# One decoder layer on one core: the input projection issued in a written order, slot by slot, on all five queues

## The chip, the core and the metric

The kernel runs on one core of a Trainium2 chip. A core has a matrix engine (PE, with a weight load that overlaps it, PEld), a vector engine (DVE), a scalar engine (ACT), GpSimd (POOL) and SyncE (SP); SP and POOL issue most of the DMAs. Each engine takes its own instructions strictly in order and waits on semaphores for the others. The metric is the device time of one execution in microseconds, as the median of several runs; lower is better.

## The reference, cut to what matters

One layer: a normalised input `h` is projected to 7168 columns, which feed a convolution branch and a recurrence branch; both are gated, merged, projected and added to the input; a squared-ReLU MLP and a last normalisation follow. Sequence 1024, model width 1024, float32.

```python
z = jnp.einsum("bsd,de->bse", rms_norm(x, g_mix), w_in) + b_in
va, ga, xb, gb, sa, sb = jnp.split(z, cuts, axis=-1)   # 1024,1024,1536,1536,1024,1024
u = causal_depthwise_conv(va * jax.nn.sigmoid(ga), conv_a_w, conv_a_b)   # width 31
y_a = silu(layer_norm(u, ln_g, ln_b)) @ w_a_out
v = causal_depthwise_conv(xb, conv_b_w, conv_b_b)                        # width 4
v = rg_lru(v, ...)       # two block-diagonal gates of 16 heads of 96, then a scan in position
y_b = (v * gelu(gb)) @ w_b_out
m = sigmoid(sa) * y_a + sigmoid(sb) * y_b
x = x + m @ w_o
x = x + square(relu(rms_norm(x, g_mlp) @ w_1)) @ w_2
return rms_norm(x, g_final)
```

## The kernel before, in words

**Numbers.** Every matrix product is made of three passes in a reduced float format: each operand is split into a high and a low part, and high*high, high*low and low*high are accumulated. A low part is made in one of two ways: `split` (L54) copies on ACT and subtracts on DVE; `split_dma` (L67) writes minus the source on ACT (L69), adds the source by an accumulating POOL DMA (L70), and copies the high part on ACT (L71).

**Stages, in order of time.** (1) The opening normalises `x` and computes the first three column chunks (of 128 columns) of the projection (L305 to L372, an order written by hand). (2) The rest of the first 28 chunks: 12 of `xb`, 8 pairs `va`/`ga`; this is `zchunk` (L384), 48 matmuls of 128x128 by 128x512 for each of 25 chunks, called from the loop L597. Beside it run the recurrence: width-4 convolution (`xb_chunk`, L399), split (`rnn_load`, L423), 16 heads with 12 matmuls each (`rnn_gates`, L443), exponentials, tanh, roots and the scan (`rnn_scan`, L464); and the width-31 convolution `conv` (L522), some 48 DVE instructions for each of eight tiles. (3) The other 28 chunks, `gb`, `sa`, `sb`, in 14 pairs; each pair is a 2x2 block product with seven block products instead of eight (L637 to L743): `z_load` brings two raw tiles, `z_lhs` forms the sums on DVE and splits them, `z_mm` does 12 matmuls, `z_out` applies gelu or sigmoid. That is 98 steps, in the order `zseq` (L727). The right-hand sums (`x_sums`, `x_parts`) are prepared at the end of stage 2. (4) `yb` (L816), the layer normalisation (L780), `ya` (L830), the output projection, the MLP up (L1103, L1239) and down (L1310) stages and the last rows.

**What sets the order.** Where the code stands in `manual_schedule` (the opening, the start of the up stage, the down stage) PE, ACT and DVE issue in the order of the program text. Everywhere else, stages 2 and 3 among them, the library's scheduler orders each queue: it simulates the program with its timeline model (`schedule_with_timeline_sim=True`, L1486) and issues by priority what is ready in that model; `high_priority` (L402, L455, L508, L705) and `high_priority(-LOWP)` (L541) move the priorities.

**Memory.** Activations take 35 tiles of 4 KB a partition (`acts`, L36). Stage 2 has pools for weights (L42), heads (L126) and head weights (L127), in this order of addresses; stage 3 opens its pools (L621 to L625) over the same addresses: eight tiles of 4 KB for raw and split weights, then sums, then evacuated blocks. In PSUM stage 2 has three tiles of two banks for chunks and two of one bank for the heads.

Of the kernel before, what the change touches and what calls it, by code (L numbers as in the profile page):

```python
# [9 lines left out]
F32 = mybir.dt.float32  # L10
# [5 lines left out]
P = 128  # L16
# [14 lines left out]
def trunk_kernel(ctx: ExitStack, tc: tile.TileContext, x, xt_in, vecs, w_in, w_a_out, w_b_out,  # L31
# [4 lines left out]
    tp = ctx.enter_context(tc.tile_pool(name="acts", bufs=35))  # L36
# [5 lines left out]
    wp = stage.enter_context(tc.tile_pool(name="weights", bufs=2))  # L42
# [7 lines left out]

    def PS2(name):
        return pp.tile([P, HS], F32, tag="half", name=name, bufs=2)
# [73 lines left out]
    qp = stage.enter_context(tc.tile_pool(name="heads", bufs=6))  # L126
    rp = stage.enter_context(tc.tile_pool(name="head_w", bufs=2))  # L127

# [3 lines left out]
    def H(name, dt=F32):  # L132
        return qp.tile([HD, S], dt, tag="h", name=name)
# [29 lines left out]
    def load_w0(i):  # L163
        if i < 2:
            raw0.append(load_w(w_in[16 + i], f"w{i}"))
        else:
            raw0.append(T(f"w{i}_raw").rearrange("p (k c) -> p k c", c=P))
            nc.sync.dma_start(raw0[i], w_in[16 + i])
# [52 lines left out]
    def x_spread(hf):  # L221

        rb[hf] = PS2(f"rb{hf}")
# [81 lines left out]
    with tc.manual_schedule(engines={mybir.EngineType.Activation, mybir.EngineType.DVE,  # L305
# [15 lines left out]
        x_root(0, lambda: first_w(0, "h"))  # L321
        x_spread(0)
# [59 lines left out]
    zc = [0]  # L382

    def zchunk(ci):  # L384
        zc[0] += 1
        if zc[0] <= N0:
            return z0[zc[0] - 1]
        ws = get_w(w_in[ci], f"win{ci}", 100 if zc[0] < 5 else None)
        ps = PS(f"z{ci}")
        mm3(ps, [w + xw[k] for k, w in enumerate(ws)])  # L390
        return ps
# [7 lines left out]
    def xb_chunk(t):  # L399
        ps = zchunk(XB + t)  # L400
        a = T(f"xb{t}")
        with tc.high_priority():  # L402
            nc.scalar.activation(a, ps, AF.Identity, bias=bin_c[:, XB + t:XB + t + 1])  # L403
# [4 lines left out]
        for d in range(1, WB):  # L408

            w = WB - 1 - d  # L410
            nc.vector.scalar_tensor_tensor(v[:, d:S], a[:, 0:S - d],  # L411
                                           cbw_c[:, w * 12 + t:w * 12 + t + 1], v[:, d:S],
                                           ALU.mult, ALU.add)
        vt[t] = v
# [8 lines left out]
    def rnn_load(n):  # L423

        g, hh = divmod(n, 4)
        parts[n] = H(f"vh{n}", F32R), H(f"vl{n}", F32R)
        for (ti, p0, p1, d0) in PIECES[hh]:
            t = 3 * g + ti
            if t not in vp_:
                vp_[t] = T(f"vth{t}", F32R), T(f"vtl{t}", F32R)  # L430
                split(vt[t], *vp_[t])
# [54 lines left out]
    def rnn_steps():  # L486
        for n in range(-2, NH):
            if n >= 0:
                rnn_gates(n)
# [1001 lines left out]
```

## Time and profile before

| | |
|---|---|
| median of 3 runs | 1679.08 us (1678.63 to 1680.56) |
| the profiled execution | 1677.35 us |
| its span, first to last instruction | 1675.6 us |
| PE busy in it | 1588.4 us, 6910 matmuls |
| DVE, ACT, POOL busy | 1114.5, 886.3, 205.9 us |
| mean granted PE clock | 0.98 |

A matmul overlaps the next one, so a busy PE is not yet a PE at its pace: what counts is how long a stretch takes against its number of matmuls. "Idle before" is the time in which an engine stood still ahead of an instruction, with what ended it. Times in the views count from the start of the span.

### The profile page before, as it was taken

To read this page: it belongs to the slowest core of one execution; us is meant where nothing else is said; L and a number is where in the kernel's file an instruction comes from. 1 tells how busy PE (TensorE), PEld (TensorE's weight loads), DVE (VectorE), ACT (ScalarE), POOL (GpSimd) and SP (SyncE) were. 2 spreads that over 40 slices of the span, in tenths; PEclk is the share of its full clock that TensorE was granted. 3 is DMA by queue.
4 is the path that set the end of the run, shared out by engine and by line. 5 is a ranking of instruction groups with operands and counts; after the bars stand their busy time and mean duration, and the time that the engine had idled before them with its cause. 6 is when DMAs were issued, how large, how long until landed. Compare 5 with 4: busy or idle time off the path is not lost.

```text
span 1675.6 us, 18924 instructions
## 1 busy us (share of the span) xinstructions
PE 1588.4 (95%) x6910; PEld 1291.3 (77%) x6910; DVE 1114.5 (67%) x1488; ACT 886.3 (53%) x1184; POOL 205.9 (12%) x276
## 2 busy tenths in 40 slices
PE   8997989996899999999999999999999999999997
PEld 6875767774677777878788888788888888888875
DVE  6785988686998983324633224875555467888896
ACT  5548776583555656633553315654444466555542
POOL 0000000001222333311111100000000001111110
PEclk9998999998899999999999999999999999999999
DMA  9657776858578778857577542532333569888852
GB/s 368 159 138 205 185 189 174 219 146 244 124 185 230 199 197 227 213 175 219 133 207 176 150 157 89 158 126 102 125 113 114 161 232 235 214 222 209 209 113 101
DMA packets 97710, 299.15 MB, mean 179 GB/s; under 512 B 11424, under 2 KB 12960, under 8 KB 97616
## 3 DMA queue, kind: packets, MB, share of 16 engines
q1 hardware_dynamic: 62832, 193.36, 34.7%
q0 software_dynamic: 34640, 104.32, 28.8%
q8 instruction: 54, 0.88, 0.2%
q14 instruction: 40, 0.33, 0.1%
q10 hardware_dynamic: 144, 0.26, 0.0%
HBM read 146.11 MB, written 54.53 MB: 120 GB/s over the span
## 4 chain that ended last, share of the span: by engine, by line
PE 62%; issue 11%; DMA 8%; ACT 4%; DVE 3%; POOL 1%; SPq 0%; POOLq 0%; ACTq 0%; DVEq 0%
PE d L1275 13%; PE ya L95 5%; PE yb L95 4%; PE o L874 3%; PE e L1390 3%; PE z L95 3%; PE keep L1275 2%; PE o L95 2%; DMA zo<-zs 2%; DMA zo<-zw 1%; DMA g<-g 1%; PE o L898 1%; DMA yn<-yd 1%; DMA win_l<-win_raw 1%; DMA wb2a_raw<-in_w_b_out_dram 1%
## 5 line engine op out<-in xcount | busy, mean ns | idle before, releaser
L95 PE MATMUL z<-xh,win_h 128*128 128x512 f32 x400 | 125.1, 391 | 3.0 <-ACT xb L403 2.1
L95 PE MATMUL z<-xl,win_h 128*128 128x512 f32 x400 | 124.3, 391 | 0.0
L1287 DVE TENSOR_TENSOR acc<-acc,d 128x1024 f32<-128x1024 f32 x72 | 87.7, 1220 | 33.4 <-PE d L1275 32.8
L95 PE MATMUL z<-xh,win_l 128*128 128x512 f32 x400 | 99.2, 401 | 4.0 <-DMA win_l<-win_raw 4.0
L95 PEld LDWEIGHTS z<-xh,win_l 128*128 128x128 f32 x400 | 77.8, 195 | 21.3 <-DMA win_l<-win_raw 4.4
L95 PEld LDWEIGHTS z<-xh,win_h 128*128 128x128 f32 x400 | 74.8, 188 | 21.1 <-ACT xb L403 2.6
L95 PEld LDWEIGHTS z<-xl,win_h 128*128 128x128 f32 x400 | 75.4, 189 | 16.4
L548 DVE SCALAR_TENSOR_TENSOR y<-u,vec,y 128x498 f32<-128x498 f32 (+14 forms) x120 | 86.5, 740 | 0.3 <-ACT y L539 0.3
L548 DVE SCALAR_TENSOR_TENSOR yt<-u,vec,yt 128x499 f32<-128x499 f32 (+13 forms) x112 | 83.0, 741 | 0.0
L548 DVE SCALAR_TENSOR_TENSOR y<-yt,csum,y 128x499 f32<-128x499 f32 (+13 forms) x112 | 82.9, 740 | 0.0
L456 ACT ACTIVATE g<-rg,vec 96x512 f32<-96x512 f32 x64 | 41.3, 678 | 42.2 <-PE rg L454 17.3
L70 POOL DMA_DIRECT2D win_l<-win_raw x25 | 21.5, 859 | 333.2 <-ACT win_l L69 273.6
L1008 ACT ACTIVATE o<-s 128x512 fp32r<-128x512 f32 x64 | 38.1, 621 | 32.5 <-DVE s L1000 27.8
L1008 ACT ACTIVATE o<-w_raw 128x512 fp32r<-128x512 f32 x40 | 24.9, 624 | 51.2 <-DVE o L922 51.2
L411 DVE SCALAR_TENSOR_TENSOR v<-xb,vec,v 128x1023 f32<-128x1023 f32 (+2 forms) x36 | 45.7, 1279 | 5.0 <-ACT v L406 4.7
L823 DVE TENSOR_TENSOR m<-yb,sb 128x1024 f32<-128x1024 f32 x8 | 9.8, 1223 | 55.9 <-PE yb L95 55.9
L70 POOL DMA_DIRECT2D db_1l<-wr x7 | 6.0, 859 | 330.4 <-ACT db_1l L69 269.6
L452 PE MATMUL rg<-vh,rgh 96*96 96x512 f32 x64 | 27.9, 435 | 18.7 <-ACT g L456 18.6
L922 DVE TENSOR_TENSOR o<-s,o 128x512 fp32r<-128x512 f32 x64 | 42.4, 684 | 3.8 <-ACT o L1008 3.8
L906 DVE TENSOR_TENSOR x<-xr,o 128x1024 f32<-128x1024 f32 x8 | 9.7, 1219 | 51.9 <-PE o L874 37.7
L70 POOL DMA_DIRECT2D zo<-zw x42 | 36.4, 866 | 37.0 <-ACT zo L69 34.0
L121 ACT ACTIVATE xn<-x 128x1024 f32<-128x1024 f32 x8 | 8.5, 1057 | 58.8 <-DVE x L906 58.8
(1586 smaller groups left out, 4694.2 us busy)
## 6 DMA issues: line engine op xcount, KB each, us to landing
fr<-fd SPq DMA_DIRECT2D x32, 512.0 KB, 5.4
wr<-in_w_dram SPq DMA_DIRECT2D x32, 512.0 KB, 5.3
w_raw<-in_w_dram SPq DMA_DIRECT2D x31, 512.0 KB, 3.7
zw<-in_w_in_dram SPq DMA_DIRECT2D x28, 512.0 KB, 5.7
win_raw<-in_w_in_dram SPq DMA_DIRECT2D x25, 512.0 KB, 4.5
win_l<-win_raw POOLq DMA_DIRECT2D x25, 512.0 KB, 4.9
zo<-zw POOLq DMA_DIRECT2D x42, 256.0 KB, 4.1
fd<-fa SPq DMA_DIRECT2D x16, 512.0 KB, 3.3
```

Of the source, the lines that this page charges most:

```text
L70: nc.gpsimd.dma_start(l, src, accum_op=ALU.add)
L95: nc.tensor.matmul(ps[:, HALVES[hf]], a, b[hf], start=i == 0, stop=i == len(todo) - 1)
L411: nc.vector.scalar_tensor_tensor(v[:, d:S], a[:, 0:S - d], cbw_c[:, w * 12 + t:w * 12 + t + 1], v[:, d:S], ALU.mult, ALU.add)
L452: nc.tensor.matmul(o, gh[:, gi, :], vh[:, hs], start=True, stop=False)
L456: nc.scalar.activation(a[:, hs], o, AF.Sigmoid, bias=(ba_c, bx_c)[gi][:, n:n + 1])
L548: nc.vector.scalar_tensor_tensor(o[:, k:], a[:, 0:HS - k], c, o[:, k:], ALU.mult, add)
L874: nc.tensor.matmul(ps[:, HALVES[hf]], tok(a, k, t), wo[k][b][:, HALVES[hf]], start=k == 0 and b == 0 and n == 0, stop=k == 7 and b == 1)
L922: tt(l, src, h.bitcast(F32), ALU.subtract)
L1008: nc.scalar.activation(o[:, 0], src, AF.Copy)
L1275: nc.tensor.matmul(o, a, b, start=n == 0 and (p != 1 or g == 0), stop=n == len(todo) - 1, skip_group_check=p == 1 and g > 0)
L1287: tt(acc[p, q2], acc[p, q2], ps, ALU.add)
L1390: nc.tensor.matmul(o, a, b, start=n == 0, stop=n == len(todo) - 1)
```

## The change

Stages 2 and 3 are written as two loops inside `manual_schedule` for all five engines. Stage 2 is a loop over 25 slots, one chunk each. A slot issues: the load of the chunk after next; 36 of the 48 matmuls; the first gate of the previous head and the matmuls of its second gate; the other 12 matmuls; the first-gate matmuls of the next head; then the evacuation of the previous chunk, the split of the next chunk's weights, and the pieces of scan, sums and head loads that the tables assign to the slot. A small planner adds up costs written in the code for PE, ACT and DVE (`clk`) and places DVE work that must wait (`later`) and the taps of the width-31 convolution (`fill`) into the gaps of the DVE order. Stage 3 is a loop over the 98 steps with the same planner: the output of step n-1, the matmuls of step n, the weight split of step n+3 and the sums of step n+4.

Other parts: the opening computes `xb` 0, `va` 0, `ga` 0 instead of `xb` 0, 1, 2; a head's gate is one tile of two banks and one ACT instruction of 96x1024 instead of two halves, and there is one such tile; all low parts of stage 3 go by DMA (two of seven went by DVE), four of the eight right-hand low parts too; the weights pool moves behind the heads in the address order; 37 activation tiles instead of 35, made room for by half the descriptor scratch; taps that are left run inside `yb`, and the two steps of the layer normalisation move from `yb` chunks 2 and 4 to 4 and 5; the timeline model is switched off, so what lies outside of written orders (`yb`, `ya`, output projection, most of the up stage, the end) is ordered by the library's other, default model.

```diff
-    tp = ctx.enter_context(tc.tile_pool(name="acts", bufs=35))
+    tp = ctx.enter_context(tc.tile_pool(name="acts", bufs=37))
...
-    qp = stage.enter_context(tc.tile_pool(name="heads", bufs=6))
+    qp = stage.enter_context(tc.tile_pool(name="heads", bufs=4))
     rp = stage.enter_context(tc.tile_pool(name="head_w", bufs=2))
+    wp = stage.enter_context(tc.tile_pool(name="weights", bufs=2))
...
-            raw0.append(load_w(w_in[16 + i], f"w{i}"))
+            raw0.append(load_w(w_in[(16, 0, 8)[i]], f"w{i}"))
...
+    def fill(until):
+        while clk["V"] + 0.74 <= until:
...
+            if next(taps["now"], None) is None:
...
+    def dve(cost, ready, f, *a):
+
+        fill(ready)
+        f(*a)
+        return at("V", cost, ready)
...
+    def head_mm(n, gi):
+        vh, vl = parts[n]
+        gh, gl = gws[n]
+        gps[n, gi] = ps = PS(f"rg{n}_{gi}", "ps2")
...
+    def scan_root(g):
+        at("A", 2.56)
+        for t in range(3 * g, 3 * g + 3):
+            r = gate[0, t]
+            nc.scalar.activation(r, r, AF.Sqrt)
+            rooted[t] = at("A", 1.06)
...
+    HS0 = [5 + 5 * (n // 4) + n % 4 for n in range(NH)]
+    head_at = {s: n for n, s in enumerate(HS0)}
...
+    with tc.manual_schedule(engines=ENGINES):
+        for s in range(3, NC1):
+            w_load(s + 2)
+            begun = clk["P"]
+            clk["A"], clk["V"] = max(clk["A"], begun), max(clk["V"], begun)
+
+            chunk_mm(s, 0, 18)
+            before, new, nxt = (head_at.get(s + d) for d in (-1, 0, 1))
+            if before is not None:
+
+                head_gate(before, 0, begun)
+                head_mm(before, 1)
+            chunk_mm(s, 18, 24)
+            if new is not None:
+                head_mm(new, 0)
+
+            c = CH[s - 1]
+            if s == 3:
+                xb_out(0, zps[0])
+            if c >= XB:
+                xb_out(c - XB, zps[s - 1])
+            elif c >= GA:
+                u_out(c - GA, zps[s - 2], zps[s - 1])
+            w_parts(s + 1)
...
+            if before is not None:
+                head_gate(before, 1, clk["P"] - 12 * MM)
...
+            vector_work(clk["P"] - 0.7)
+            if nxt is not None:
+                head_load(nxt)
...
         o = wp.tile([P, 2, 4, P], F32R, tag="w", name=f"zo{i}_{p}")
-        if p in (7, 3):
-            nc.scalar.activation(o[:, 0], src, AF.Copy)
-            nc.vector.tensor_tensor(o[:, 1], src, o[:, 0].bitcast(F32), ALU.subtract)
-        else:
-            split_dma(src, o[:, 0], o[:, 1])
+        split_dma(src, o[:, 0], o[:, 1])
...
+    with tc.manual_schedule(engines=ENGINES):
+        z_load_to(4)
+        for n in range(4):
+            z_get(n, z_sums)
+        vector_work(clk["V"])
+        for n in range(3):
+            z_get(n, z_lhs)
+        u_out(7, zps[NC1 - 2], zps[NC1 - 1])
+        vector_work(clk["V"])
+        for n in range(len(zseq) + 2):
+            z_load_to(n + 8)
+            clk["A"], clk["V"] = max(clk["A"], clk["P"]), max(clk["V"], clk["P"])
+            z_get(n - 1, z_post)
+            z_get(n - 2, z_post2)
...
+            z_get(n, z_mm)
+            z_get(n + 3, z_lhs)
+            z_get(n + 4, z_sums)
+            for f, *a in ZX.get(n, ()):
+                f(*a)
+            vector_work(clk["P"] - 0.3)
...
-        if j in (2, 4):
+
+        fill(clk["V"] + 13.5 if j < 4 else math.inf)
+        if j in (4, 5):
             next(ln_it, None)
...
-    nc = _bacc.Bacc("TRN2", target_bir_lowering=False, num_devices=1)
+    nc = _bacc.Bacc("TRN2", target_bir_lowering=False, num_devices=1,
+                    dynamic_dma_scratch_size=8192)
...
-    with _tile.TileContext(nc, schedule_with_timeline_sim=True) as tc:
+    with _tile.TileContext(nc) as tc:
```

468 lines of the change are left out of this document (275 added, 193 removed).

## The prediction

> **What bounds the kernel now.** I first read the busy time of each engine stretch by stretch. Each row gives the stretch, its length, busy time and instructions of PE, PEld, DVE, ACT and POOL, then the granted PE clock, DMA share and GB/s.
>
> ```profile
> span 1675.6 us, 18924 instructions
> ...
> 51.20:406.40 355.20, 329.50 (x1394) 260.89 (x1392) 277.51 (x349) 226.70 (x253) 26.58 (x33) 0.96 0.70 182
> 406.40:419.50 13.10, 0.21 (x1) 0.00 (x1) 3.83 (x4) 5.04 (x7) 1.55 (x3) 0.68 0.93 296
> 419.50:717.40 297.90, 278.48 (x1170) 223.91 (x1171) 226.52 (x346) 176.33 (x300) 90.63 (x124) 0.96 0.76 199
> 717.40:857.90 140.50, 137.27 (x595) 111.03 (x594) 57.03 (x45) 54.99 (x59) 20.05 (x28) 1.00 0.58 169
> 857.90:945.30 87.40, 87.40 (x387) 72.34 (x386) 35.29 (x36) 34.59 (x41) 12.31 (x17) 1.00 0.68 182
> ...
> 1348.00:1615.00 267.00, 265.33 (x1167) 217.99 (x1165) 215.69 (x186) 157.86 (x160) 40.08 (x47) 1.00 0.82 212
> ```
>
> PE is the bound, and the measure is a stretch's length against its matmuls. In `ya` (857.9 to 945.3) the code has 8 chunks of 48 matmuls, 384 in 87.4 us: 0.2276 us each. The down stage (1348 to 1615), whose order is written by hand (L1310), has 49 steps of 24, 1176 in 267.0 us: 0.2270. That is PE at its pace; I use 0.227. Stage 2 has 25 chunks of 48 and 16 heads of 12 matmuls, 1392, which at that pace take 316.0 us; it takes 355.2, so 39.2 are lost. Between the stages 13.1 are lost. Stage 3 has 98 steps of 12, 1176, or 267.0 us; it takes 297.9, so 30.9 are lost. The sum, **83.2 us**, is all that an order can win there. `yb` has 576 matmuls, 130.8 us, in 140.5.
>
> Next come PE's waits, longest first (total, times, longest):
>
> ```profile
> PE rg L452 <- ACT g L456: 18.6, 6, 5.5
> ...
> PE z0a L683 <- ACT zo L71: 12.9, 1, 12.9
> ```
>
> The two name the places. This is the timeline of one of the waits of the heads, with start and length:
>
> ```profile
> 155.96 1.28 ACT L456 ACT_TABLE_LOAD   x1
> ...
> 157.99 0.74 PE L452 MATMUL rg<-vh,rgh 96*96 96x512 f32 x1 [5.52 <-ACT g L456]
> ...
> 158.53 0.63 PE L453 MATMUL rg<-vh,rgl 96*96 96x512 f32 x1
> ...
> 158.78 1.28 ACT L477 ACT_TABLE_LOAD   x1
> ...
> 158.95 0.63 PE L454 MATMUL rg<-vl,rgh 96*96 96x512 f32 x1
> ...
> 162.09 1.28 ACT L456 ACT_TABLE_LOAD   x1
> ...
> 178.79 3.79 PE L95 MATMUL z<-xh,win_l 128*128 128x512 f32 x16
> ```
>
> ACT changes its table three times in 6 us, because the order mixes sigmoids and roots, while PE waits 5.52 us for a bank that a sigmoid must empty. Afterwards the matmuls start 0.42 us apart (158.53, 158.95), in place of 0.227 as in the row of 16, which took 3.79 us. A stall of this length is paid again in matmuls at half pace. [...]
>
> The gap between the stages:
>
> ```profile
> 406.54 2.10 SPq L640 DMA_DIRECT2D zw<-in_w_in_dram  x4
> ...
> 414.46 1.06 ACT L585 ACTIVATE xs<-xs 128x1024 f32<-128x1024 f32 x1 [8.80 <-DMA xs<-xu]
> ...
> 418.31 0.62 ACT L69 ACTIVATE zo<-zw 128x512 fp32r<-128x512 f32 x1
> ...
> 419.50 0.79 PE L683 MATMUL z0a<-xh,zo 128*128 128x512 f32 x1 [12.89 <-ACT zo L71]
> ```
>
> The raw tiles of stage 3 are requested at 406.54, after the last chunk's matmuls, since its pool lies over stage 2's weights; ACT stands 8.80 us ahead of a right-hand sum, and the split that z0 needs follows at 418.31.
>
> **The change part by part.** *Matmuls.* Their number is the same: the dense time of both stages stays 583.0 us, and the question is which stalls remain.
>
> *Stage 2.* The gates get one PSUM tile. The first gate's tile is free after ACT's first instruction of the slot, 8.2 us (36 matmuls) before it is used again; the second's must be emptied within 12 matmuls, 2.7 us, for which ACT needs about 1.1 us. Whether ACT is on time follows from its work in a slot:
>
> ```profile
> L456 ACT ACTIVATE g<-rg,vec 96x512 f32<-96x512 f32 x64 | 41.3, 678 | 42.2 <-PE rg L454 17.3 <-DMA g<-g 16.1 <-PE rg L453 7.5
> ...
> L403 ACT ACTIVATE xb<-z,vec 128x1024 f32<-128x1024 f32 x12 | 13.3, 1105 | 8.2 <-PE z L95 8.2
> ...
> L406 ACT ACTIVATE v<-xb,vec 128x1024 f32<-128x1024 f32 x12 | 14.8, 1237 | 0.1
> ...
> L69 ACT ACTIVATE win_l<-win_raw 128x1024 fp32r<-128x1024 f32 x25 | 26.3, 1052 | 17.2 <-PE z L95 13.4 <-PE z L260 3.9
> ...
> L473 ACT ACTIVATE a<-g,c 128x1024 f32<-128x1024 f32 x12 | 13.4, 1147 | 0.1
> ...
> L474 ACT ACTIVATE g<-g,sm 128x1024 f32<-128x1024 f32 x12 | 13.7, 1140 | 0.1
> ...
> L477 ACT ACTIVATE g<-g 128x1024 f32<-128x1024 f32 x12 | 12.5, 1055 | 0.1
> ```
>
> The gate of 96x1024 isn't in the trace; it lies between one half (0.68) and two (1.36), and I take 1.1, as in L403's row for the same length. The fullest slot is that behind a group's last head: two gates 2.2, an `xb` chunk 1.105 and 1.237, a weight split 2.1 (twice L69's 1.05), a `v` copy of the same size 1.05, a table load 1.28, three times 1.147 and 1.140: 15.8 us against 12.3 of PE (54 matmuls). The next has 2.34, 2.1, 1.05, two loads 2.56 and three roots 3.17: 11.2 of 12.3. The third has 5.4 of 13.6. ACT is some 3.5 us late for one slot, in which no head is waiting for a bank, and then recovers. DVE has 277.5 us in 355.2 now and must do somewhat more, for convolutions start earlier. They fill what is free, at a planned 0.74 us a tap:
>
> ```profile
> 399.34 0.73 DVE L548 SCALAR_TENSOR_TENSOR y<-u,vec,y 128x499 f32<-128x499 f32 x1
> 399.99 0.74 DVE L548 SCALAR_TENSOR_TENSOR yt<-u,vec,yt 128x499 f32<-128x499 f32 x1
> ```
>
> but taps start 0.65 us apart, so the plan holds 12% in hand there. On SP a chunk's weights stand behind the gates' copies and the scans' stores of the slot before, but are asked for two slots, over 20 us, ahead of use. I charge stage 2 with 8 us. The bounds are 0, as in the down stage, whose order is written too, and the 39.2 of now; the down stage is the nearer row, but here fifteen head banks and late pieces of `v` cross the order.
>
> *Between the stages.* The pool of raw tiles now lies over the heads, which end four slots earlier, so its loads no longer wait for weights. But they stand on SP behind the last two scans' stores, and those behind some 9 us of DVE in the last slot of 10.9. Bounds: nothing, and today's 13.1. Load and low part take about 12 us from there (406.54 to 418.31 now), PE has 2 us left, so some 10 stay, or less where the first of four loads lands ahead of the others; I take 9.
>
> *Stage 3.* The pace now, and the landing times of the low parts:
>
> ```profile
> L683 PE MATMUL z5a<-xh,zo x16: 387/390/501, 526.6 to 547.2; 128*128 128x512 f32 x16
> ...
> L683 PE MATMUL z6a<-xh,zo x16: 389/389/514, 552.5 to 570.1; 128*128 128x512 f32 x16
> ...
> L683 PE MATMUL z12a<-xh,zo x16: 389/389/389, 673.1 to 689.2; 128*128 128x512 f32 x16
> ...
> L683 PE MATMUL z13a<-xh,zo x16: 389/389/389, 692.1 to 707.7; 128*128 128x512 f32 x16
> ```
>
> ```profile
> DMA to landing us min/median/max: 3.2/3.9/8.5
> ```
>
> From z12 to z13 seven steps take 19.0 us, the dense value (84 x 0.227 = 19.07), so the pool of eight tiles can carry it; from z5 to z6 they take 25.9. In the change the split for step n+3 is issued when step n begins: up to three evacuations of 128x512, 1.9 us at L69's 0.63 below, the negated copy, 0.63, then the DMA. The low part is read by the third matmul, 3 x 2.72 + 0.45 = 8.6 us after that beginning; so a landing of 6.1 us is free, and the median is 3.9, the longest 8.5. When the next pair's raw tiles are in, only three split tiles are free and the lead shrinks to two steps, 5.9 us against 2.5 + 3.9. On POOL the DMA also stands behind the store of the last product, which waits for DVE, by one or two taps of 0.65. A few stalls of under a us remain in each pair: I charge 9 (bounds 0 and 30.9). The two low parts per pair that move to DMA:
>
> ```profile
> L663 DVE TENSOR_TENSOR zo<-zs,zo 128x512 fp32r<-128x512 f32 x28 | 19.1, 688 | 9.5 <-ACT zo L662 9.4
> ...
> L69 ACT ACTIVATE zo<-zs 128x512 fp32r<-128x512 f32 x28 | 17.6, 630 | 28.8 <-DMA zo<-zw 11.8 <-DVE zs L649 8.0 <-DVE hb L696 5.1
> ...
> L70 POOL DMA_DIRECT2D zo<-zs x28 | 24.1, 860 | 97.3 <-ACT zo L69 90.9 <-DVE zs L649 4.8 <-DVE hgl L56 1.6
> ```
>
> They take 19.1 us from DVE and add 28 negated copies of 0.63 us to ACT (176.3 of 297.9 us busy) and 28 issues of 0.86 to POOL (90.6 of 297.9): neither gets full. If that cover went, ACT's 17.6 us would count. The four right-hand low parts (1024 wide, 1.05 us of ACT each) stand where ACT has room as well. DVE, the other candidate, has 504 us in both stages now, 485 after, in 583. Half the descriptor scratch I set at nothing, bounds 0 and the whole 30.9 of stage 3: POOL's issues take 0.86 us at nearly every place, so no row shows one that waits for room, and nothing is the nearer end. Two more activation tiles and the other first chunks (three as before) cost nothing; the first convolution only starts earlier.
>
> *Outside.* The layer normalisation moves:
>
> ```profile
> L788 DVE TENSOR_TENSOR yn<-yn,mu x8: 1211/1216/1222, 775.5 to 791.6; 128x1024 f32<-128x1024 f32 x8
> ...
> L55 ACT ACTIVATE suh<-yn x8: 1040/1042/1061, 838.2 to 864.2; 128x1024 fp32r<-128x1024 f32 x8
> ```
>
> The first of its sums began at 775.5, behind the third `yb` chunk, and `suh` was ready at 838.2, 62.7 us later, for a `ya` that began at 857.9. The sums now stand behind the fifth chunk, two chunks of 16.35 us (72 matmuls) later; with the same 62.7 us `suh` comes at 870.9, 13 us late. Part of the 62.7 was a wait of the second step for the fifth chunk, which now overlaps. The default model orders all that isn't written: its bounds are a gain of `yb`'s 9.7 us and, here, the loss of 13. I take 5, between them.
>
> *Sum.* 1675.6 - 83.2 + 8 + 9 + 9 + 5 = 1623.4 us of span. The profiled execution has 1677.35 for a span of 1675.6, so 1625.2; the median of the runs is 1.7 above it: **1627 us**.
>
> **The rivals.** *Half of it.* The written order trades one kind of stall for another: a gate that ACT empties late holds the only gate tile, PE waits, then runs at half pace. For: 18.6 us of such waits now, with two banks; against: the slot's ACT sum. If each of the 16 heads lost 2 us (32 us) the time is 1659. I give 1645 to 1672.
>
> *Slower.* One mechanism: in stage 3 a low part that comes late stops PE at every step, since nothing else may be put in its place. With ACT's 2.5 us and the longest landing, 8.5, in place of the median, a step lasts (11.0 - 0.45) / 3 = 3.5 us, 0.8 over 2.72; 98 steps cost 78 instead of 9: 1696 us. To be slower by 0.2% (3.4 us, about what a measurement of this kernel can tell from no change) the losses must exceed 86.6, which needs 0.66 us a step, a mean landing of 8.1 us. The 28 further DMAs and a DMA share of 0.76 speak for it, the median against.
>
> *Won here, lost outside.* Only two stretches are newly written out. From 717.4 to 1348 and from 1615 on, 691 us, the default model takes over. If it lost 7.5% there, about what `yb` loses now (9.7 of 140.5), the 52 us of gain are gone: no change, near 1679. Against it: `ya` and what follows are dense now, with PE in program order.
>
> **How the numbers follow.** Forecast (1604 to 1645) 0.62; half 0.18; under 1604, if stages 2 and 3 run as the down stage does, 0.04; within 0.2% 0.03; slower 0.13. The likeliest is 1627. The range 1604 to 1672 holds the first two, 0.80, and so the bounds of stage 2, the gap and `yb`. Faster by over 0.2%: 0.62 + 0.18 + 0.04 = 0.84; same 0.03; slower 0.13.
>
> **What would show it.** Right: no PE wait for a gate over 1 us, 36 matmuls of a chunk in one piece, 13.6 us a slot with a head; a granted clock of 0.98 or more in stages 2 and 3; seven steps in 19 to 20 us; the raw tiles requested before stage 2's last matmul. Wrong: PE waits for `zo` DMAs in most steps, DVE behind the planner with PE waiting for `u`, or stretches outside longer than now by more than 10 us.

## The result, and the profile after

The changed kernel takes **1655.38 us** (median of 3 runs, 1651.43 to 1659.51), 0.9857 of the time before (95% interval 0.9817 to 0.9897): 23.7 us faster, where 52 were forecast. Its profiled execution took 1651.43 us, with a span of 1649.7. Here are the stretches of the changed kernel, divided where its own stages begin (columns as in the first view of the prediction):

```profile
51.70:369.50 317.80, 317.80 (x1393) 256.24 (x1392) 261.52 (x324) 198.68 (x204) 27.88 (x32) 1.00 0.79 201
369.50:377.70 8.20, 0.06 (x1) 0.00 (x0) 1.19 (x1) 5.99 (x7) 2.88 (x4) 0.80 1.03 304
377.70:430.10 52.40, 38.78 (x148) 30.52 (x149) 22.35 (x30) 28.44 (x46) 15.94 (x20) 0.80 0.84 197
430.10:677.60 247.50, 238.35 (x1033) 192.47 (x1033) 160.84 (x240) 163.54 (x283) 101.55 (x134) 1.00 0.94 241
...
677.60:838.80 161.20, 142.95 (x586) 113.16 (x585) 103.43 (x116) 57.09 (x62) 21.02 (x29) 0.94 0.53 151
838.80:927.80 89.00, 88.96 (x385) 73.06 (x386) 35.33 (x36) 34.84 (x41) 10.98 (x14) 0.98 0.66 187
...
1597.80:1649.70 51.90, 43.68 (x193) 35.86 (x191) 44.29 (x90) 13.03 (x42) 0.00 (x0) 0.95 0.28 100
```

Stage 2 (51.7 to 369.5) is dense: 1392 matmuls in 317.8 us against 316.0. The gap takes 8.2 us. Stage 3 (377.7 to 677.6) takes 299.9 us and `yb` (677.6 to 838.8) 161.2. The prediction ends stage 3 of the kernel before at 717.4, but its last step only starts at 717.1, and `yb` at 720.8:

```profile
L95 PE MATMUL yb<-hgh,wb0h x24: 389/389/507, 720.8 to 742.2; 128*128 128x512 f32 x24
```

So stage 3 took 301.3 us before and `yb` 137.1; the earlier boundary counted 3.4 us of stage 3 to `yb`. The table goes by 720.8.

| | before | after | loss after, against dense | charged |
|---|---|---|---|---|
| stage 2 | 355.2 | 317.8 | 1.8 | 8 |
| gap | 13.1 | 8.2 | 8.2 | 9 |
| stage 3 | 301.3 | 299.9 | 32.9 | 9 |
| `yb` and `ya` | 224.5 | 250.2 | (25.7 more) | 5 for all outside |
| the end, from 1615 and 1597.8 | 60.6 | 51.9 | (8.7 less) | 0 |

The opening (51.2, then 51.7) and the stretch from `o` to the down stage (about 670 us in both) did not move. Stage 3 splits in two. Before:

```profile
419.50:462.20 42.70, 35.91 (x137) 27.88 (x138) 42.36 (x66) 23.46 (x40) 10.05 (x13) 0.86 0.54 125
462.20:720.80 258.60, 245.19 (x1046) 197.88 (x1044) 185.63 (x284) 154.47 (x264) 81.12 (x112) 0.98 0.80 214
```

The first twelve steps (dense 32.7 us) took 42.7 us before and take 52.4 now; the other 86 (dense 234.3) took 258.6 and take 247.5. So the steps from z2 on did gain 11.1 us, and the start gave 9.7 of them back. The pairs in the middle run at pace, the last do not:

```profile
L822 PE MATMUL z5a<-xh,zo x16: 389/389/389, 492.0 to 505.4; 128*128 128x512 f32 x16
...
L822 PE MATMUL z12a<-xh,zo x16: 387/389/496, 626.7 to 644.0; 128*128 128x512 f32 x16
...
L822 PE MATMUL z13a<-xh,zo x16: 389/389/499, 649.6 to 665.2; 128*128 128x512 f32 x16
```

From z5 (492.0) to z12 (626.7) 49 steps take 134.7 us, against 133.5 dense. From z12 to z13 (649.6) seven steps take 22.9 us, against 19.1. Of the 13.2 us that the 86 steps lose, 4.7 lie ahead of z5, 1.2 between z5 and z12, and 7.3 behind z12. PE's longest waits name the other places:

```profile
PE z0a L822 <- DMA zo<-zw: 11.5, 1, 11.5
PE z0a L822 <- ACT zo L67: 8.2, 1, 8.2
PE ya L91 <- ACT suh L51: 7.8, 1, 7.8
...
PE yb L91 <- ACT hgh L51: 4.0, 2, 3.7
```

No wait for a gate is left. Now the start of stage 3 in order of time:

```profile
355.89 15.14 SPq L530 DMA_DIRECT2D hd<-g  x3
...
371.08 2.54 SPq L779 DMA_DIRECT2D zw<-in_w_in_dram  x4
...
377.44 0.87 POOL L66 DMA_DIRECT2D zo<-zw  x1 [2.35 <-ACT zo L65]
...
377.72 0.80 PE L822 MATMUL z0a<-xh,zo 128*128 128x512 f32 x1 [8.16 <-ACT zo L67]
...
388.53 1.28 DVE L413 SCALAR_TENSOR_TENSOR u<-z,vec,u 128x1024 f32<-128x1024 f32 x1 [17.85 <-ACT u L540]
...
390.43 1.22 PE L822 MATMUL z0a<-xh,zo 128*128 128x512 f32 x2 [11.48 <-DMA zo<-zw]
```

SP holds the stores of the last three scans (`hd`) for 15 us, so the raw tiles `zw` are asked for at 371.08, after stage 2's last matmul. The first low part's DMA is issued at 377.44; PE goes on at 390.43, 13.0 us later, at half pace (1.22 us for two matmuls, 0.62 in stage 2; a granted clock of 0.50 until 394.0). And DVE, which has taps to do, stands 17.85 us behind one instruction: it waits for an ACT instruction that the written order puts behind three splits, which wait for `zw`.

How long each part of this wait lasts is not firm. In the six other kernels below whose edits do not aim at this start (`tap065`, `ln24`, `tap_ln`, `zlow_dve`, `after_timeline`, `scratch4k`) PE stands 8.5 to 16.7 us ahead of z0, and the first low part takes 5.2 to 13.9 us from its issue until PE goes on. Its end moves less: PE goes on at 390.6 to 394.1, and z2 begins at 428.1 to 432.0.

The late start of `ya`, on DVE:

```profile
752.02 1.23 DVE L602 TENSOR_TENSOR ysum<-ysum,y 128x1024 f32<-128x1024 f32 x1
...
772.36 1.23 DVE L1008 TENSOR_TENSOR m<-yb,sb 128x1024 f32<-128x1024 f32 x1 [15.10 <-PE yb L91]
774.07 1.22 DVE L973 TENSOR_TENSOR yn<-yn,mu 128x1024 f32<-128x1024 f32 x1 [0.49 <-PE mu L968]
```

The last tap of the width-31 convolution and its sum end at 753.3, inside `yb` (before: 639.6). The sums of the layer normalisation stand behind the fifth `m`, though the taps have long ended by then, and PE stands 7.8 us for `suh` ahead of `ya`.

### The profile page after: what moved, and what is told of

Read it like the earlier page. It is cut to its first block, busy times and chain, and to the rows that moved or that the text cites. A ratio compares the mean times of both kernels' runs of the same rounds, so it can differ in the third digit from the quotient of the medians.

```text
span 1649.7 us, 18943 instructions
## 1 busy us (share of the span) xinstructions
PE 1581.7 (96%) x6910; PEld 1289.5 (78%) x6910; DVE 1096.1 (66%) x1456; ACT 875.5 (53%) x1168; POOL 235.5 (14%) x306
## 4 chain that ended last, share of the span: by engine, by line
PE 74%; issue 9%; DMA 9%; DVE 4%; ACT 2%; POOL 1%; POOLq 0%; SPq 0%; ACTq 0%; DVEq 0%
PE z L686 14%; PE d L1462 14%; PE ya L91 5%; PE o L1061 3%; DMA zo<-zw 2%; PE e L1577 2%; PE keep L1462 2%; DMA zo<-zs 2%; PE o L91 2%; PE z L257 2%; PE rg L485 1%; PE rg L487 1%; PE rg L486 1%; POOL zo L66 1%; PE o L1085 1%
## 5 line engine op out<-in xcount | busy, mean ns | idle before, releaser
L1474 DVE TENSOR_TENSOR acc<-acc,d 128x1024 f32<-128x1024 f32 x72 | 87.8, 1220 | 33.3 <-PE d L1462 32.7
L588 DVE SCALAR_TENSOR_TENSOR y<-u,vec,y 128x511 f32<-128x511 f32 (+14 forms) x120 | 88.4, 737 | 0.0
L493 ACT ACTIVATE g<-rg,vec 96x1024 f32<-96x1024 f32 x32 | 35.7, 1114 | 96.7 <-PE rg L487 58.6
L588 DVE SCALAR_TENSOR_TENSOR y<-yt,csum,y 128x511 f32<-128x511 f32 (+6 forms) x112 | 82.6, 737 | 0.0
L588 DVE SCALAR_TENSOR_TENSOR yt<-u,vec,yt 128x511 f32<-128x511 f32 (+6 forms) x112 | 82.6, 737 | 0.0
L66 POOL DMA_DIRECT2D zo<-zs x56 | 50.2, 906 | 75.4 <-ACT zo L65 73.8
L1255 ACT ACTIVATE fa<-fa 128x512 f32<-128x512 f32 x16 | 10.1, 631 | 89.9 <-DVE fa L1233 89.9
L65 ACT ACTIVATE zo<-zs 128x512 fp32r<-128x512 f32 x56 | 35.0, 626 | 29.6 <-issue 15.6
L91 PE MATMUL ya<-suh,wa_h 128*128 128x512 f32 x128 | 40.3, 398 | 7.8 <-ACT suh L51 7.8
L1109 DVE TENSOR_TENSOR o<-w_raw,o 128x512 fp32r<-128x512 f32 x40 | 27.5, 689 | 29.2 <-ACT o L1195 29.2
```

What stands on the lines that cost most here:

```text
L65: nc.scalar.activation(l, src, AF.Copy, scale=-1.0)
L66: nc.gpsimd.dma_start(l, src, accum_op=ALU.add)
L91: nc.tensor.matmul(ps[:, HALVES[hf]], a, b[hf], start=i == 0, stop=i == len(todo) - 1)
L493: nc.scalar.activation(a, gps.pop((n, gi))[:HD, :], AF.Sigmoid, bias=(ba_c, bx_c)[gi][:, n:n + 1])
L588: nc.vector.scalar_tensor_tensor(o[:, k:], a[:, 0:HS - k], c, o[:, k:], ALU.mult, add)
L1109: tt(l, src, h.bitcast(F32), ALU.subtract)
```

## The experiments

Theories at the outset: in stage 3, **D**, the transfers are full, against **Q**, the place of the raw tiles' loads on SP; in `yb`, **T**, taps left over, against **L**, the place of the layer-normalisation steps; at the end, **O**, the ordering model. Fifteen kernels were run; ratios are to the kernel before, with the 95% interval. The intervals are 0.2 to 0.3% to each side, the changed kernel's own 0.9817 to 0.9897; what is smaller is read from the traces.

### Layer normalisation and taps

```diff
 ln24 (on the changed kernel)
-        fill(clk["V"] + 13.5 if j < 4 else math.inf)
-        if j in (4, 5):
+        fill(clk["V"] + 13.5 if j < 2 else math.inf)
+        if j in (2, 4):
```

> The two steps of the layer normalisation stand behind the third and the fifth yb chunk again (as before the change) in place of the fifth and the sixth, and the rest of the taps is issued behind the third chunk. Theory L (place): the first sum begins some 30 us earlier, suh no longer comes 7.8 us late for ya, yb falls by about 11 us to 150, the time to about 1644. Theory T (left-over taps): the sums need the last convolution, which ends at 752, so the mean's matmuls make PE wait there; yb keeps 155 to 165 and the time stays at 1650 to 1660.

1641.86 us, 0.9776 (0.9756 to 0.9795). The mean's matmuls and the first product of `ya` in this kernel (durations in ns, then first and last start):

```profile
L968 PE MATMUL mu<-ysum,onesm x4: 592/592/677, 752.1 to 753.4; 128*128 128x512 f32 x4
```

```profile
L91 PE MATMUL ya<-suh,wa_h x128: 387/389/499, 828.4 to 912.2; 128*128 128x512 f32 x128
```

The mean is taken at 752.1, right behind the last tap, and `ya` begins at 828.4 in place of 838.8; `yb` takes 150.0 us in place of 161.2. Theory L holds in size; theory T sets the floor that it now meets.

```diff
 tap065 (on the changed kernel)
-        while clk["V"] + 0.74 <= until:
+        while clk["V"] + 0.65 <= until:
...
-        def step(cost=0.74):
+        def step(cost=0.65):
```

> The planner counts a convolution tap at 0.65 us (the pitch that the traces show) in place of 0.74; everything else as in the changed kernel. Theory T (yb is 20.7 us longer because one convolution and a half are left over when stage 3 ends, and hold DVE, the activation tiles and the sums of the layer normalisation): 14% more taps go into the two stages, some 40 of the 380, the last convolution ends near 725 us in place of 752, yb falls from 161 to about 145 and the time by 10 to 16 us, to 1640 to 1645. Theory L (it is the place of the layer-normalisation steps alone): yb stays within 4 us of 161 and the time at 1652 to 1657. Theory D (stage 3 is bound by DMA, not by what the planner thinks of DVE): stage 3 stays at 300 us either way; if DVE were really full, stage 3 would grow by 5 us or more.

1656.91 us, 0.9862 (0.9837 to 0.9887): no change. The last tap and the mean:

```profile
L602 DVE TENSOR_TENSOR ysum<-ysum,y x7: 1218/1224/1226, 214.0 to 710.2; 128x1024 f32<-128x1024 f32 x7
...
L968 PE MATMUL mu<-ysum,onesm x4: 590/592/594, 774.4 to 775.7; 128*128 128x512 f32 x4
```

The taps end 42 us earlier, more than expected, and nothing follows, since the mean still stands behind the fifth chunk. Stage 3 ends at 678.5: DVE had the room. Both edits together (`tap_ln`):

> The planner's tap at 0.65 us and the layer-normalisation steps behind the third and fifth yb chunk, together. The first alone ended the last tap at 711 us in place of 753 and changed no time (the mean's matmuls stayed at 774, behind the fifth chunk); the second alone gave 15 us (mean at 752, right behind the last tap). Theory: each of the two holds what the other would free, so together the mean's matmuls come at about 740, behind the third chunk, suh is ready near 812, yb lasts until 815 to 820 (678 + 130.8 dense + 8 to 10 us of waits for hg and wb1), and the time is 1629 to 1634. Rival (the chain from the mean to suh, 76 us with the second edit, sets the start of ya whatever ends when, since it gets longer when it lies beside more of yb's splits): the mean is 12 us earlier but ya only a few; 1637 to 1642.

1636.58 us, 0.9751 (0.9727 to 0.9774).

```profile
L968 PE MATMUL mu<-ysum,onesm x4: 590/592/594, 739.0 to 740.3; 128*128 128x512 f32 x4
```

```profile
L91 PE MATMUL ya<-suh,wa_h x128: 387/389/398, 824.1 to 907.0; 128*128 128x512 f32 x128
```

The mean is taken at 739.0, 13 us earlier than with the one edit, and `ya` begins at 824.1, 4.3 earlier: between the theory and its rival. The gain over `ln24` lies within the intervals of the times; the trace shows it. Place first, taps second.

### The transfers

```diff
 xlow_dve (on the changed kernel)
-            if c2 == 0:
+            if c2 < 0:
 
 zlow_dve (on the changed kernel)
-        split_dma(src, o[:, 0], o[:, 1])
-        at("A", 1.24)
+        if p in (7, 3):
+            nc.scalar.activation(o[:, 0], src, AF.Copy)
+            later(at("A", 0.62), 0.69, nc.vector.tensor_tensor, o[:, 1], src,
+                  o[:, 0].bitcast(F32), ALU.subtract)
+        else:
+            split_dma(src, o[:, 0], o[:, 1])
+            at("A", 1.24)
```

> The four right-hand low parts of the first half of the contraction are subtracted by DVE (as those of the second half) instead of by accumulating DMA; the rest as in the changed kernel. Theory D (the first steps of stage 3 lose 20 us because the transfers are full at the end of stage 2, with the accumulating 512 KB DMAs among them): the DMA share at 360 to 390 us falls, the first low part lands in about 8 us in place of 13, gap and first twelve steps together lose some 20 us in place of 28, and the time falls by 4 to 8 us, to 1647 to 1651. Theory Q (the raw tiles are asked for behind the stores of the last scans, and that alone sets the start): zw is still requested near 371 us, the first product of stage 3 still starts near 378 and pauses until 390, and the time stays at 1653 to 1658; DVE's 5 us more in the last slots could make it 2 us worse.

> Two of the seven left-hand low parts of each pair of stage 3 are subtracted by DVE again, as before the change; the rest as in the changed kernel. Theory D (the DMA share of 0.92 in stage 3 is what the 28 further accumulating DMAs brought, and they cost the pace): the share falls to about 0.85, seven steps fall from 19.5 to 19.1 us, the loads of hg at the end no longer hold the last pairs, and stage 3 falls by 5 to 10 us. Rival (DMA has room in the steady pairs, as 19.0 to 19.7 us for seven steps show; the loss is at the start, where only a few of the 28 stand): stage 3 changes by under 3 us, and DVE's 19 us more push some 29 taps out of stage 3 into yb, which grows by 5 us or more: 1653 to 1662 in all.

`xlow_dve`: 1650.96 us, 0.9829 (0.9812 to 0.9845), which overlaps the changed kernel's. Its stage 3, first twelve steps and the rest:

```profile
379.80:423.40 43.60, 37.27 (x148) 29.75 (x149) 22.25 (x30) 28.42 (x46) 15.94 (x20) 0.87 0.83 190
423.40:676.30 252.90, 239.65 (x1034) 192.20 (x1034) 160.19 (x239) 163.96 (x283) 100.97 (x134) 1.00 0.91 231
```

z2 starts at 423.4 in place of 430.1, but the other 86 steps take 252.9 us in place of 247.5, and `yb` begins at 676.3 in place of 677.6: the start is won and given back. `zlow_dve`: 1659.72 us, 0.9879 (0.9862 to 0.9895).

```profile
428.10:667.80 239.70, 235.95 (x1033) 193.16 (x1032) 158.38 (x242) 147.62 (x256) 81.48 (x111) 1.00 0.78 206
667.80:845.90 178.10, 148.31 (x586) 115.67 (x584) 122.40 (x142) 61.09 (x66) 21.06 (x29) 0.90 0.55 160
```

Here the 86 steps take 239.7 us, 5.4 over dense, and `yb` begins at 667.8, 10 us earlier; but the last tap ends at 783, `yb` takes 178.1 us, and the whole is not faster. The queues and the split DMAs of stage 3 in the changed kernel (q0 is POOL's queue, with the accumulating DMAs; packets, MB, share of the 16 engines):

```profile
q0 software_dynamic: 18871, 41.47, 63.6%
q1 hardware_dynamic: 9627, 28.23, 28.4%
...
zo<-zs POOLq DMA_DIRECT2D x56, 256.0 KB, 4.9
```

and without 28 of the accumulating DMAs:

```profile
q0 software_dynamic: 15306, 35.61, 51.2%
q1 hardware_dynamic: 8849, 25.37, 27.0%
...
zo<-zs POOLq DMA_DIRECT2D x28, 256.0 KB, 3.8
```

From z2 on the share fell from 0.94 to 0.78, and the landing of `zo<-zs` from 4.9 to 3.8 us. Of the 7.8 us gained there, 2.4 lie ahead of z5 (487.6 here), 4.3 behind z12 (621.2), and only 1.1 in the seven pairs between. So theory D holds at the two ends, and the rival is right about the steady pairs, as well as about the taps that DVE's work pushes into `yb`. The edit also took 28 negated copies from ACT and 28 issues from POOL (from z2 on ACT is busy for 147.6 us in place of 163.5, POOL for 81.5 in place of 101.6); no run separates these from the transfers. The two theories meet in the kernels that also end the taps and the layer normalisation early:

> As the kernel with the tap at 0.65 us and the earlier layer-normalisation steps, and only the four right-hand low parts of the first half on DVE. Theory D: z2 starts some 6 us earlier (422 to 424), but with all left-hand low parts by DMA the share stays above 0.88 and yb still begins at 675 to 678: 1634 to 1639, no change against 1636.6. Theory S (the jam is only at the start, and what is won there stays, once the taps no longer hold the end): yb begins near 671, and the time is 1628 to 1632.

> Tap at 0.65 us, layer-normalisation steps behind the third and fifth yb chunk, and besides these the low parts put back on DVE in both places: two of seven left-hand ones in each pair and the four right-hand ones of the first half. Theory D (what stage 3 loses is transfer time: yb began at 676 to 678 us in every kernel with all low parts by DMA, whether z2 started at 423 or at 432, and at 668 with 28 fewer): the DMA share in stage 3 is about 0.77, z2 starts near 423, seven steps take 19.1 us, and yb begins at 658 to 664; the taps that 24 us more of DVE push out end near 735, the mean comes at 735 to 740, suh near 815, the time is 1618 to 1627. Rival (DVE's 24 us cost what the transfers give): the last tap ends behind 750 us as with the two low parts alone (782 there, with a tap at 0.74), the mean too, and the time is 1634 to 1642.

`tap_ln_x` (`tap_ln` with the right-hand edit): 1631.10 us, 0.9718 (0.9690 to 0.9745), `yb` from 668.3. `combo` (both low-part edits): **1626.65 us**, 0.9684 (0.9662 to 0.9706), `yb` from 662.5, its last taps at 735. `tap_ln_x` went against theory D, which had left no gain at `yb`'s start: z2 began at 421.0 (428.3 in `tap_ln`), and the gain stayed; its own 86 steps lose 13.0 us like the changed kernel's 13.2. `xlow_dve`'s give-back is thus not settled.

### The start of stage 3

```diff
 hd_pool (on the changed kernel), combo_hd (on combo)
-        nc.sync.dma_start(hd[t], i)
+        (nc.gpsimd if t >= 9 else nc.sync).dma_start(hd[t], i)

 combo_def (on combo)
-        nc.sync.dma_start(hd[t], i)
+        last_hd.append((hd[t], i)) if t >= 9 else nc.sync.dma_start(hd[t], i)
...
-        z_load_to(4)
+        z_load_to(4); [nc.sync.dma_start(o, i) for o, i in last_hd]
```

> The stores of the last three scans go out on POOL's queue in place of SP's, so that the raw tiles of stage 3 no longer stand behind them on SP; the rest as in the changed kernel. Theory Q (the place on SP sets the start): zw is requested 8 to 12 us earlier (near 360 in place of 371), the first splits run by 370, the gap goes from 8.2 to 2 or 3 us, the first twelve steps from 52.4 to below 42, and z2 starts at 412 to 420 in place of 430. Theory D (the transfers are full from 310 to 390, with the accumulating DMAs among them): zw is requested earlier but lands only a few us earlier, what it gains the right-hand sums lose, and z2 starts at 426 to 430. In either case what is gained here need not reach the end: without the accumulating right-hand parts z2 started 6.7 us earlier and stage 3 ended only 1.3 us earlier; so the time is 1650 to 1657.

1652.74 us, 0.9843 (0.9823 to 0.9864). `zw` was asked for at 360.2, and z2 started at 426.6, 3.5 us earlier than in the changed kernel and 1.5 earlier than in any of the six kernels named above: as theory D has it, for the right-hand sums lost what the raw tiles gained. ACT waited for one of these sums ahead of the first split, which then began at 378.50 without a wait for `zw`:

```profile
373.75 1.06 ACT L630 ACTIVATE xs<-xs 128x1024 f32<-128x1024 f32 x1 [10.46 <-DMA xs<-xu]
```

> The kernel with four edits (tap at 0.65 us, earlier layer-normalisation steps, two left-hand low parts per pair and four right-hand ones on DVE) and, on top, the stores of the last three scans on POOL's queue. In the changed kernel the same move of the stores asked for zw 10.8 us earlier and won only 3.5 us at z2, since the accumulating transfers stood in the way. Theory DQ (two causes in a row: with the transfers relieved, the place of zw behind the stores on SP is what sets the start, for ACT waits 9.6 us for zw there and for nothing else): zw is asked for near 360 and split by 370, z2 starts at 411 to 415 in place of 420.9, and the time is 1617 to 1622. Rival (the raw tiles' transfers cannot go faster, or the low parts then stand behind the stores on POOL): z2 starts at 418 or later and the time stays at 1624 to 1629.

1621.17 us, 0.9648 (0.9620 to 0.9676). z0 began 0.5 us after stage 2, but z2 at 418.2, on the rival's side. On POOL:

```profile
372.29 0.56 POOL L530 DMA_DIRECT2D hd<-g  x1 [4.08 <-DVE g L529]
372.89 3.68 POOL L66 DMA_DIRECT2D zo<-zw  x4
```

The first low part stood behind a store that waited 4.08 us for the last scan. So:

> The kernel with the four edits, and the stores of the last three scans written behind the loads of the first raw tiles on SP (in place of ahead of them), none on POOL. With the stores on POOL, zw came 10.7 us earlier and z0 began 0.5 us after stage 2, but the first low part's DMA stood on POOL behind a store that waited for the last scan (issued 372.9, landed 381.4), and z2 came only 2.7 us earlier. Theory DQ (the place of the stores, first on SP, then on POOL, is what holds the start): zw is asked for near 361, the first low part is issued by 370 and lands by 376, z2 starts at 409 to 414 and the time is 1613 to 1620. Rival (the landing itself is what takes long there, with the transfers full): the first low part lands 8 us or more after its issue, z2 stays at 416 to 421 and the time at 1619 to 1628.

**1619.00 us**, 0.9630 (0.9609 to 0.9650), the fastest of all: 36 us under the changed kernel, 61 under the one before on its chip. The first low part on POOL, PE when it has landed, and the two stretches of 10 us:

```profile
370.72 0.87 POOL L66 DMA_DIRECT2D zo<-zw  x1 [1.54 <-ACT zo L65]
```

```profile
379.66 1.22 PE L827 MATMUL z0a<-xh,zo 128*128 128x512 f32 x2 [7.92 <-DMA zo<-zw]
```

```profile
370.00:380.00 10.00, 1.29 (x4) 0.64 (x4) 9.20 (x9) 7.18 (x11) 4.36 (x5) 0.72 1.05 290
380.00:390.00 10.00, 10.00 (x35) 8.04 (x35) 3.52 (x6) 4.84 (x7) 0.87 (x1) 0.77 1.09 255
```

Issued 6.7 us earlier than in the changed kernel, it still took 8.9 us, with the transfer engines full (1.05, 1.09): z2 at 416.8, the rival. Of the 27.9 us lost between stage 2's end and z2 in the changed kernel 14.0 stay here. The queue order is worth some 4 us here (z2 at 420.9 in `combo`), the four right-hand low parts 7 (`tap_ln` against `tap_ln_x`); the rest is not settled. No kernel put the first splits ahead of the right-hand sums in ACT's order.

### The written orders

```diff
 free_st2: the loop of stage 2; free_st3: the loop of stage 3 (on the changed kernel)
-    with tc.manual_schedule(engines=ENGINES):
+    with contextlib.nullcontext():
```

> The changed kernel with the code of stage 2 in its new order, but ordered by the default model instead of as written (stage 3 stays as written). If the written order is what took 37 us out of stage 2, the waits for the one gate bank come back: stage 2 takes 350 to 370 us in place of 317.8, and the time is 1685 to 1710. Rival (the new order of the code, the single gate tile, the earlier first pair and the 37 tiles do it, and the default model keeps to them as it keeps PE dense in ya): stage 2 takes under 330 us and the time stays within 10 us of 1655.

1667.23 us, 0.9926 (0.9903 to 0.9950). But not in stage 2. Its first and last rows of matmuls, and the wait of the projection ahead of them:

```profile
L686 PE MATMUL z<-xh,win_h x400: 389/389/398, 64.7 to 378.1; 128*128 128x512 f32 x134
...
L686 PE MATMUL z<-xh,win_l x400: 387/389/398, 72.0 to 382.1; 128*128 128x512 f32 x134
```

```profile
PE z L257 <- ACT xh L228: 12.4, 2, 12.3
```

From 64.7 to 382.3 it is 317.6 us, as dense as the written one. It is not the default model by itself: under it the kernel before takes 364.6 us from the first to the last start of these matmuls (`before_default`, 52.0 to 416.6), this one 317.4. The stage only starts 13.0 us later (51.7 in the changed kernel), since in the opening the high part of `x` now came 12.3 us late. The rival is right about the stage: what removed the waits for gates is how the code is arranged (slots, one gate tile and the rest), not that the order is binding. Which of these, was not separated.

> The changed kernel with the code of stage 3 as it is, but ordered by the default model (stage 2 stays as written). The kernel before, ordered by the default model, needed 293 us from z0 to yb, with two of seven low parts on DVE; the changed one needs 299.9 as written. Theory D (in stage 3 the written order is not what decides, the transfers are): z0 to yb takes 290 to 305 us and the time is 1645 to 1665. Rival (the written order does win there, and the transfers only hide it): without it z0 to yb takes 310 us or more, the time 1668 or more.

1687.88 us, 1.0048 (1.0029 to 1.0067): slower than before the change. Stage 3:

```profile
385.50:713.50 328.00, 288.50 (x1180) 229.20 (x1181) 186.80 (x279) 189.14 (x326) 117.02 (x153) 0.95 0.82 210
```

328.0 us in place of 299.9. The expectation from theory D fails: for this code of stage 3 the written order does win, 28 us. (Without it the code has no priorities either, which the kernel before gave to its evacuations.) What else the change brought there takes nearly as much away, for stage 3 took 301.3 us before the change, and 293.1 in `before_default`, which has neither the written order nor the new code. Some 10 us of it go with the 28 added low parts by DMA, as `zlow_dve` shows.

### The ordering model and the scratch

```diff
 before_default (on the kernel before)
-    with _tile.TileContext(nc, schedule_with_timeline_sim=True) as tc:
+    with _tile.TileContext(nc) as tc:

 after_timeline (on the changed kernel): the reverse
 scratch4k (on the changed kernel)
-                    dynamic_dma_scratch_size=8192)
+                    dynamic_dma_scratch_size=4096)
```

> The kernel before the change with one edit: what is not written by hand is ordered by the default model, as in the changed kernel, not by the timeline model. Theory O (the end of the program, 60.4 us before and 51.9 after, is the ordering model's doing): the stretch behind the down stage falls to about 52 us. For the stages that were not written there, one of two: the timeline model was worth something, then stage 2, the gap and stage 3 take more than 355 + 13 + 298 us (670 to 700 in all), and the time is 1670 to 1710; or it was worth nothing, then they stay at 666 and the time is near 1671 (8.5 us less than before). Rival to theory O (the end is shorter because something that the change moved, a tile or a queue, is free earlier): the end stays at 60 us.

> The changed kernel with the timeline model for what is not written by hand. Theory O: the end takes about 60 us again, 8 more than 51.9. The opening, yb and ya are ordered by it too: if the default model costs something in yb (theory L of the layer normalisation says that only the place counts), yb changes by 5 us or more; otherwise it stays at 161 to 163 and the time is near 1662. Rival: no stretch changes by more than 2 us, 1652 to 1658.

`before_default` 1678.32 us, 0.9989 (0.9974 to 1.0005); `after_timeline` 1656.46 us, 0.9861 (0.9840 to 0.9882). From the start of the down stage to the end, with the timeline model (before, then `after_timeline`):

```profile
1348.00:1675.60 327.60, 312.14 (x1371) 256.12 (x1369) 262.25 (x275) 171.82 (x202) 40.10 (x47) 0.99 0.72 189
```

```profile
1328.50:1657.10 328.60, 313.11 (x1369) 257.12 (x1367) 261.80 (x275) 171.76 (x202) 40.15 (x47) 0.98 0.72 188
```

and with the default model (`before_default`, then the changed kernel):

```profile
1356.50:1675.00 318.50, 310.36 (x1369) 256.16 (x1367) 260.09 (x275) 171.91 (x202) 40.59 (x47) 1.00 0.74 195
```

```profile
1331.10:1649.70 318.60, 310.38 (x1369) 256.20 (x1367) 259.62 (x275) 172.05 (x202) 40.59 (x47) 0.99 0.74 194
```

Theory O is shown: 9 to 10 us go with the model, whatever the rest. Ahead of that the model was worth about as much the other way: in `before_default` `ya` began at 865.8 in place of 858.3. In `after_timeline` `yb` took 147.7 us in place of 161.2 and stage 3 4.6 more. So switching the model off cost the changed kernel 13.5 us in `yb` and gave 10 at the end. Two edits, this one and `ln24`, thus each take 11 to 14 us out of `yb`; they were not combined, and how much they overlap is open.

> The descriptor scratch at 4096 bytes in place of 8192, everything else as in the changed kernel; the change itself halved it from 16384. As set in the prediction (halving costs nothing): POOL's issue of a low part stays at 0.87 us everywhere and the time within 0.2% of the changed kernel's (ratio to before 0.984 to 0.988). Rival (the room for descriptors is a limit, and the change already paid for a part of it): POOL's issues wait for room, some of them take over 2 us, stage 3 grows by 5 us or more and the time passes 1660.

1651.77 us, 0.9835 (0.9811 to 0.9859): no loss. POOL's issues of the 42 low parts of raw tiles, in the changed kernel and with half its scratch:

```profile
L66 POOL DMA_DIRECT2D zo<-zw x42 | 36.5, 868 | 59.1 <-ACT zo L65 54.1 <-ACT zo L67 1.7 <-PE z9a L822 1.2
```

```profile
L66 POOL DMA_DIRECT2D zo<-zw x42 | 36.5, 869 | 62.0 <-ACT zo L65 53.4 <-DMA zw<-in_w_in_dram 6.3 <-ACT zo L67 1.7
```

## Why the prediction was right and wrong, by its own steps

**Stage 2, 8 us: too much by 6.** The mechanism held (no gate wait is left, ACT recovers), and the nearer row, the dense down stage, was the right one. `free_st2` adds that the binding order was not needed for it.

**The gap, 9 us: the number came out (8.2), in part by luck.** The reason holds: the loads stand on SP behind the last scans' stores. But they were asked for 1.6 us after stage 2's end, not 2 us ahead of it, and z0 began 6.6 us after that, not some 12. Those 12 us (406.54 to 418.31) end at the first split, so the landing of the low part, which the prediction names there, was not in them. Nor is 8.2 firm: in the six kernels named above PE stands there for 8.5 to 16.7 us.

**Stage 3, 9 us: the step that failed** (32.9). It read "a landing of 6.1 us is free, and the median is 3.9" from the traffic of before. But the change itself adds accumulating DMAs, and starts stage 3 while others are under way. The median over all low parts is only 4.4 now, but the longest, 12.9, is that of the first one, for which PE stands 11.48 us:

```profile
DMA to landing us min/median/max: 3.2/4.4/12.9
```

The sum had a steady pace only, and in the 49 steps from z5 to z12 that pace holds: they lose 1.2 us. The loss stands at the two ends of the stage, for which the sum had no term: 19.7 of the 32.9 us in the first twelve steps, 4.7 from there to z5, and 7.3 behind z12. That it is the transfers is shown for a part: without the four right-hand low parts by DMA z2 came 7.3 us earlier (`tap_ln_x`), and without 28 left-hand ones 6.7 us less were lost between z2 and z5 and behind z12 (`zlow_dve`). That the first low part queues is the author's reading of the engines' share, 1.03 in the gap; no run shows it by itself. The "slower" rival had this mechanism, but asked for it at every step.

**DVE, cost nothing: wrong.** "The plan holds 12% in hand" was booked as a reserve. A plan that counts 0.74 us for what takes 0.65 leaves DVE empty (183.2 us busy of 299.9), and the taps that it does not place come later. "485 of 583" said that DVE has room; it did not say that the order would use it. With the layer normalisation at its earlier place the right cost brought `ya` 4.3 us earlier (`tap_ln` against `ln24`).

**Outside, 5 us: too little, with the wrong bounds.** The loss of 13 was that of the moved steps alone, and `ln24` gives that step its size (13.5 us by the medians, 11.2 in `yb`). Left out were the taps in `yb`, and what the default model costs there (13.5 us by `after_timeline`). The gain bound, 9.7 us, held 3.4 of stage 3 by the early boundary, and missed the end, 8.7 us, which two runs put down to the ordering model.

**The sum.** Against 1623.4 us: stage 2 -6.2, gap -0.8, stage 3 +23.9, outside +9.4, which is the span of 1649.7. Outside is 12.8 us above the charge, less the 3.4 that the sum held twice by the early boundary. The median of the runs, 1655.4, lies above the profiled execution. That it falls among the times of "half of it" (1645 to 1672) is luck: that rival's mechanism, PE waiting for gates, is absent. Of the signs of being right, the raw tiles requested before stage 2's last matmul and a clock of 0.98 in stage 3 (0.97 in all, 0.80 in its first twelve steps) did not come; of those of being wrong, a stretch outside longer by over 10 us did (`yb`, by 24.1).

Not settled, besides the 14 us at the start of stage 3: `yb`, which in `combo_def` still takes 150.4 us for 130.8, with waits for `hg` and `wb1` at its beginning; nothing was tried there.

## What to carry to other kernels

When an edit puts work on a queue, take the landing time from the traffic that it will meet (here a median of 4.9 us for `zo<-zs` at a share of 0.94, 3.8 at 0.78), above all at the start of a stage, where the loads of the next stage meet the stores of the last (12.9 us, at 1.03 in the gap). A written order keeps what its planner believes: a cost that is set too high (0.74 us for 0.65) was not a reserve here but idle time, and the work that was left over surfaced in the next stage (the last tap at 753.3 us, 711 with the right cost). And ask what stands in front of what: the same earlier taps were worth nothing (1656.91 us against 1655.38) until the layer normalisation could use them (1636.58 against 1641.86).

## What the runs showed of the hardware

Per megabyte the queue with the accumulating DMAs kept the transfer engines busier: in stage 3 of the changed kernel 63.6% of the engines' time for 41.47 MB (1.53% each), and 28.4% for 28.23 MB (1.01% each) on SP's. This compares mixes, not single transfers. Half the descriptor scratch, and half again, moved POOL's mean issue of the 42 low parts of raw tiles by nothing that can be seen (866 ns before the change, then 868 and 869). For the low parts of sums (28 before the change, then 56) it went from 860 ns to 906 and 919; in the changed kernel the median of these is 870 and the longest 1264. No run separates the scratch from the 28 added issues in this.
